# A reordered product list in a Gated DeltaNet stage: one z product in the front, z ahead of keys early, later first recurrences, closer inverse steps

## The chip, the core and the metric

The kernel runs on one core of a Trainium2 chip, as one launch. The metric is the device time in microseconds (us) of the whole program. TensorE does the matrix products, VectorE, ScalarE and GpSimd the work on tiles, and SyncE issues the DMAs.

## The reference, cut to what matters

One inference step of two layers, a Gated DeltaNet (GDN) mixer and an RWKV-7 mixer, over 1,104 tokens (64 sample tokens in 8 sequences of 8, 16 meta tokens, 1,024 prompt tokens) with a model width of 1,024. The change touches the GDN layer alone:

```python
proj = xn @ w_in                               # q, k, v, z and two gates
qkv, new_buf = causal_conv(qkv, conv_buf, conv_w)   # width 4, then SiLU
q, k = l2norm(q) * 128 ** -0.5, l2norm(k)      # 8 heads of 128, each for two v heads
L = where(strict, (beta * k) @ k.T * decay, 0) # per chunk and head
sol = triangular_solve(L + I, rhs)             # the inverse, block by block
v_new = u - w @ S                              # recurrence over the chunks
o = (q * exp(gc)) @ S + attn @ v_new
S = S * exp(g_last) + k_dec.T @ v_new
o = rmsnorm(o) * silu(z)                       # then the output projection
```

## The kernel before

**The work.** The tokens lie in three segments (384, 384, 336). A *product* multiplies them with one 128-column block of `w_in`. Each weight and each input is split into a high and a low part, so a product has 3 segments x 8 row blocks x 3 matmuls = 72 matmuls. There are 48 of them: for each of eight head groups j one for keys (k), one for queries (q), two for values (v) and two for the gate z.

**The slots.** `product` yields after 12 matmuls, half a segment: that is a *slot*, six per product, 288 in all. `layer0` drives the generator `products` and, behind each slot, calls whatever `gdn_events` planned for a time up to the next slot (`before`). TensorE and ScalarE run strictly in this written order (`manual_schedule`). VectorE, GpSimd and SyncE are ordered by the framework's scheduler, which takes the written order as priority.

**A convolved product** (k, q, v; `conv`) copies each segment out of PSUM on ScalarE, takes three taps and a SiLU on VectorE and stores it. **A z product** (`gdn_gate`) has one tanh on ScalarE and one VectorE operation per segment, and keeps the tile `zg`, of which there are six.

**The front of a group** (`front_events`, `gdn_prep`): decay tables by DMA (`decay`), their exponentials, the score products k k^T and their scaling on VectorE (`scores`), the 32x32 diagonal blocks through memory into `invA` (`blocks`), then 31 steps of two VectorE operations each that invert all 72 blocks at once (`steps`, `inverse32`). Then `spread`: a transposing copy, two DMAs out to memory (`g_u`, `g_t`) and DMAs back into `T1n` and `TT`. Then four merges (`merges`) that put the blocks together to 64 and 128 on TensorE; the first, `y32`, reads `T1n`.

**The recurrence of a group** (`chain_events`, `gdn_recur`): begun at slot a = `first[j]`, 26 steps at one per slot over nine tiles of 128 tokens. The merges stand at a - 6.5, a - 4.5, a - 3.5 and a - 1.5; the normalised and gated output leaves at a + 14.5 to a + 31.5, in three parts and two heads (`gdn_norm_out`), which frees `zg`.

**The order before.** Group 0's k, q, v, v fill slots -24 to 0. Then each stretch j = 1 to 7 of 36 slots is k(j), z(j-1), z(j-1), q(j), v(j), v(j), and the last two z follow. `first` is 9, 43, 78 and then every 36. In a stretch with base b, b + 18 is where q starts (`qb`). The 15 pairs of inverse steps stand one slot apart (`inv`), `spread` at a - 9.9.

Of the kernel before, what the change touches and what calls it, by code (L numbers as in the profile page):

```python
# [22 lines left out]
NEG = -1.0e30  # L23
ZF = 1
QF = 0


class Ctx:
# [7 lines left out]
class Builder:  # L36
# [589 lines left out]

    def gdn_queries(self, j, G, xh, xl, after=None):
        def dst(s):
            G.Q[s] = self.t(self.kp, [128, 384], "Q", 4)
            return G.Q[s]  # L630
        return self.product(128 * j, "q", xh, xl, self.conv(G.H, 1, j, dst), after)

# [213 lines left out]
    def gdn_recur(self, j, G):  # L846

        nc, t, gp, tc = self.nc, self.t, self.gp, self.tc
        col = self.col
        S = t(gp, [128, 2, 128], "S", 2)  # L850
        hv = lambda h: 2 * j + h
        hs = (0, 1)
        G.seg = {}
        for tg in range(9):
            s, tt = divmod(tg, 3)
            TT, bv = G.TT[s], G.bv[s]
            k, q = G.K[s][:, 128 * tt:128 * tt + 128], G.Q[s][:, 128 * tt:128 * tt + 128]
            if tt == 0:
                G.seg[s] = [], t(gp, [128, 3, 2], "ssq", 2)
            os, ssq = G.seg[s]  # L860
            o = t(gp, [128, 2, 128], "o", 6)
            os.append(o)

            e = [col[:, tg, 2, hv(h):hv(h) + 1] for h in hs]
            X, w = [t(gp, [128, 128], "X", 2) for h in hs], [t(gp, [128, 128], "w", 5) for h in hs]
# [24 lines left out]
            for h in hs:  # L890
                if tg == 0:
                    self.mm(part(h, 2), kt[64:128, h], w[h][64:128])
                else:
                    self.mm(part(h, 2), kt[:, h], w[h])
            for h in hs:
                self.mm(part(h, 0), at[:, tt, h], w[h])
            with tc.high_priority():
                for h in hs:
                    if tg == 0:
                        nc.vector.tensor_copy(S[:, h], part(h, 2))  # L900
                    else:
# [12 lines left out]
            G.squares = lambda o=o, ssq=ssq, tt=tt: [self.act(t(gp, [128, 128], "ojunk", 1, BF16), o[:, h], AF.Square, accum=ssq[:, tt, h:h + 1])  # L914
                                                     for h in hs]
            if tg == 8:
                nc.sync.dma_start(self.o["p_gdn"][0, 0, 2 * j:2 * j + 2].rearrange("h k v -> k h v"), S)
            yield

    def gdn_events(self, G, open_, gate, swap):  # L920

        self.events = {}
        base = [36 * (j - 1) for j in range(9)]
        first = [9, 43] + [base[j + 1] + 6 for j in range(2, 8)]
        for u in (-22.9, -19.4, -16.8, -16.7, -16.6):
            self.at(u, gate)
        self.at(-13, swap)
        for j in range(8):
            self.chain_events(j, G, first[j])
            if j:  # L930
                self.front_events(j, G, base[j], base[j] + 18, first[j], open_, base[j] + max(0.3, first[j - 1] - base[j] - 3.4))
            else:
                self.front_events(0, G, -24, -18, first[0], None, None)

    def at(self, u, f, *a):
        self.events.setdefault(u, []).append(lambda: f(*a))
# [58 lines left out]
    def front_events(self, j, G, b, qb, a, open_, e):  # L995

        g, at = lambda: G[j], self.at
        Sb = {}
# [3 lines left out]

        def read(h):
            self.gdn_sample_read(g(), h, [Sb[h, q] for q in (0, 1)])
        va = qb + 6
        at(b + 0.1, lambda: self.gdn_prep(j, g()))
        if j:
            at(b - 5.7, open_, j)
            at(b - 1.4, lambda: self.history_turn(g().H))
            k = max(b + 5.5, e + 4.7)  # L1010
            ed, ee, es = [e + 2 * s for s in range(3)], [k + 2 * s - 1.8 for s in range(3)], [k + 2 * s for s in range(3)]
            inv, per, kk, ss, rd = [k + 9.3 + n for n in range(15)], 2, (b + 11.8, qb + 4.2), b + 13.2, (qb + 6.4, qb + 9.9)
            sp = a - 9.9
        else:
            ed, ee, es = [-18.5, -18.4, -18.3], [-16, -15.2, -14.4], [-15.2, -14.4, -13.6]
            inv, per, kk, ss, rd = [-11.5 + n for n in range(10)], 3, (-12.2, -12.1), -12.8, (-7.6, -4.1)
            sp = -1
        for s in range(3):
            at(ed[s], lambda s=s: g().decay(s))
            for tt in range(3):  # L1020
# [1101 lines left out]
    def layer0(self, top, right, xa, xc):  # L2122
# [36 lines left out]
        self.gdn_events(G, open_, lambda: next(gate, None), swap)  # L2159

        def products():
            yield from G[0].keys(0)
            yield from self.gdn_queries(0, G[0], kh, kl, 2048)
            yield from self.gdn_values(0, G[0], 0, kh, kl, 2176)
            yield from self.gdn_values(0, G[0], 1, kh, kl, 1152)
            for j in range(1, 8):
                k = 128 * (j + 1)
                z = [4096 + 256 * (j - 1), 4224 + 256 * (j - 1)]
                va = 2048 + 256 * j
                yield from G[j].keys(z[0])  # L2170
                yield from self.gdn_gate(j - 1, G[j - 1], 0, kh, kl, z[1])
                yield from self.gdn_gate(j - 1, G[j - 1], 1, kh, kl, 128 * j)
                yield from self.gdn_queries(j, G[j], kh, kl, va)
                yield from self.gdn_values(j, G[j], 0, kh, kl, va + 128)
                yield from self.gdn_values(j, G[j], 1, kh, kl, 1024 + k if j < 7 else 4096 + 256 * 7)
            yield from self.gdn_gate(7, G[7], 0, kh, kl, 4224 + 256 * 7)
            yield from self.gdn_gate(7, G[7], 1, kh, kl)

        def before(u):
            while True:  # L2180
# [2 lines left out]
                    return  # L2183
                for f in self.events.pop(v):
                    f()
        before(-24)
        with tc.manual_schedule(engines={mybir.EngineType.PE, mybir.EngineType.Activation}):
            self.slot = -24
            for _ in products():
                before(self.slot + 1)  # L2190
                self.slot += 1
# [8 lines left out]
        free = [t(self.kp, [128, 384], n, b) for n, b in (("K", 6), ("K", 6), ("Q", 4))]  # L2200
# [341 lines left out]
```

## Time and profile before

| what | us |
|---|---|
| runs shown, median of three | 2196.59 (2194.4 to 2201.57) |
| the profiled execution, whole | 2193.46 |
| its span, first to last instruction | 2191.7 |
| mean granted TensorE clock | 0.979 |
| first key product starts | 44.9 |
| keys of group 1 start | 113.4 |
| keys of group 2, 3, 4 start | 255.3, 391.4, 510.6 |
| last two z products start | 987.1 |

The profile is of one execution. A row of a timeline gives the start, the time taken, engine, source line, operation, output <- inputs, and in brackets the idle time before it with what ended it. A row of windows gives the length of the stretch, then the busy time (and instructions) of TensorE's matmuls, its weight loads, VectorE, ScalarE and GpSimd, then the granted clock, the busy share of the DMA engines, and GB/s. A row of waits gives the waiting engine and tile, the releaser, the sum in us, how often and the longest. A row of groups gives the count, the busy time, the mean in ns of one, and the idle time before. Tile names carry the kernel's names: `rY` is a merge product, `dk`, `dq`, `dv`, `dz` the projections, `E` a decay table, `invT` and `invtmp` the inverse, `cvy` the convolution.

### The profile page before, as it was taken

The page shows a single profiled execution, that of the slowest core. Times are in us where ns is not written, and L with a number is a line of the kernel's source. Part 1 is how long each engine was busy: PE and PEld are TensorE (multiplying, and loading weights), DVE is VectorE, ACT ScalarE, POOL GpSimd, SP SyncE. Part 2 cuts the span into 40 slices and gives each one's busy share as a digit, 9 for nine tenths or more (in the row PEclk, how much of TensorE's full clock was granted, in tenths as well). Part 3 has the DMA queues.
Part 4 walks back from the last instruction along what each step waited for, and adds up shares of the span by engine and source line. Part 5 has one row for each costly group of instructions (what it writes and reads, how often), then busy time and mean ns, then how long its engine had stood idle before and what let it go on. Part 6 is the DMA issues. An engine that isn't in the chain of part 4 may idle for free. (4 is left out here: it accounts for less than half of the span.)

```text
span 2191.7 us, 54812 instructions
## 1 busy us (share of the span) xinstructions
PE 2051.0 (94%) x20404; PEld 1908.7 (87%) x20404; DVE 1588.0 (72%) x4221; ACT 1291.8 (59%) x3761; POOL 844.7 (39%) x1125
## 2 busy tenths in 40 slices
PE   6869899999999999999899999889999999999997
PEld 5859799899999999999899999889888988888876
DVE  7967869788887979695334676757969657767755
ACT  5526466656566565656633365664847446777774
POOL 3423333334333333334231362344534344444444
PEclk9979999999999999999999999899999999999998
DMA  4423342333333433335345215655555376677764
GB/s 118 119 58 90 86 111 78 102 90 97 104 105 97 112 83 103 110 98 145 121 125 128 67 53 190 211 168 173 171 168 163 115 222 174 180 229 226 234 178 136
DMA packets 430661, 292.64 MB, mean 134 GB/s; under 512 B 147146, under 2 KB 412987, under 8 KB 430395
## 3 DMA queue, kind: packets, MB, share of 16 engines
q1 hardware_dynamic: 430394, 289.14, 45.9%
q8 instruction: 161, 2.64, 0.5%
q14 instruction: 106, 0.86, 0.1%
HBM read 197.68 MB, written 91.37 MB: 132 GB/s over the span
## 5 line engine op out<-in xcount | busy, mean ns | idle before, releaser
L90 POOL TENSOR_TENSOR wlo<-wraw,whi 128x512 fp32r<-128x512 f32 (+1 forms) x246 | 330.6, 1346 | 469.5 <-ACT whi L86 434.9
L76 PE MATMUL d<-xc,whi 128*128 128x384 f32 (+2 forms) x1006 | 279.7, 336 | 4.6 <-ACT whi L86 3.9
L523 DVE SCALAR_TENSOR_TENSOR cvy<-raw,cw,cvy 128x408 f32<-128x408 f32 (+2 forms) x288 | 192.5, 669 | 20.3 <-ACT cvy L62 18.8
L86 ACT CAST whi<-wraw 128x512 fp32r<-128x512 f32 (+1 forms) x246 | 149.7, 611 | 86.4 <-PE d L76 48.8
L76 PEld LDWEIGHTS d<-xc,whi 128*128 128x128 f32 (+1 forms) x1006 | 183.2, 189 | 7.4 <-ACT whi L86 4.6
L76 PE MATMUL d<-xc,wlo 128*128 128x384 f32 (+3 forms) x476 | 157.4, 339 | 2.6 <-POOL wlo L90 2.6
L76 PE MATMUL dz<-xc,whi 128*128 128x384 f32 (+1 forms) x480 | 153.7, 338 | 0.0
L76 PE MATMUL dv<-xc,whi 128*128 128x384 f32 (+1 forms) x480 | 152.2, 337 | 0.0
L76 PE MATMUL d<-xa,whi 128*128 128x384 f32 (+3 forms) x450 | 143.2, 342 | 1.6 <-DVE xb L1160 1.2
L62 ACT ACTIVATE o<-rA,gcol 128x128 f32<-128x128 f32 x128 | 42.1, 366 | 117.6 <-DVE S L902 117.3
L570 DVE TENSOR_TENSOR invtmp<-invA,invT 72x31 f32<-72x31 f32 (+15 forms) x248 | 102.5, 413 | 3.2
L76 PE MATMUL dv<-xa,whi 128*128 128x384 f32 (+1 forms) x288 | 99.0, 344 | 0.0
L572 DVE TENSOR_TENSOR invT<-invT,invtmp 72x31 f32<-72x31 f32 (+15 forms) x248 | 96.1, 388 | 3.3
L76 PE MATMUL dz<-xa,whi 128*128 128x384 f32 (+1 forms) x288 | 98.5, 342 | 0.0
L76 PEld LDWEIGHTS d<-xc,wlo 128*128 128x128 f32 (+1 forms) x476 | 89.2, 189 | 6.3 <-POOL wlo L90 3.5
L76 PEld LDWEIGHTS dz<-xc,whi 128*128 128x128 f32 x480 | 89.3, 188 | 4.6 <-issue 4.6
L76 PEld LDWEIGHTS dv<-xc,whi 128*128 128x128 f32 x480 | 89.1, 188 | 1.4 <-issue 1.4
L76 PEld LDWEIGHTS d<-xa,whi 128*128 128x128 f32 (+1 forms) x450 | 85.2, 192 | 4.8 <-issue 3.3
L76 PE MATMUL d<-xa,wlo 128*128 128x384 f32 (+3 forms) x252 | 85.6, 340 | 1.4 <-POOL wlo L90 1.4
L76 PE MATMUL dq<-xc,whi 128*128 128x384 f32 (+1 forms) x240 | 78.0, 342 | 3.0 <-ACT whi L86 3.0
L76 PE MATMUL dk<-xc,whi 128*128 128x384 f32 (+1 forms) x240 | 78.6, 347 | 0.0
L62 ACT ACTIVATE mixs<-xb,omu 128x64 f32<-128x64 f32 (+3 forms) x128 | 61.6, 521 | 18.3 <-DVE xc L90 8.6
(523 smaller groups left out, 6829.5 us busy)
## 6 DMA issues: line engine op xcount, KB each, us to landing
wraw<-in_gdn_w_in SPq DMA_DIRECT2D x96, 256.0 KB
wraw<-in_rwkv_w_rkvz SPq DMA_DIRECT2D x80, 256.0 KB
Sb<-in_state_gdn SPq DMA_DIRECT2D x64, 256.0 KB
sldcak<-cakd SPq DMA_DIRECT2D x24, 576.0 KB
wraw<-in_rwkv_w_o SPq DMA_DIRECT2D x42, 256.0 KB
E<-drow SPq DMA_DIRECT2D x24, 384.0 KB
attn<-drow SPq DMA_DIRECT2D x24, 384.0 KB
wraw<-in_gdn_w_out SPq DMA_DIRECT2D x36, 256.0 KB
```

The source lines that it names most:

```text
L62: return self.nc.scalar.activation(out, in_, func, bias=bias, scale=scale, **kw)
L76: self.nc.tensor.matmul(out, lhsT, rhs, start=start, stop=stop)
L86: nc.scalar.copy(hi, x)
L90: e.tensor_tensor(lo, x, hi.bitcast(F32), op=ALU.subtract)
L523: nc.vector.scalar_tensor_tensor(y[0][:, 0:wd], raw[:, k:k + wd], cw[k], y[0][:, 0:wd], op0=ALU.mult, op1=ALU.add)
L570: nc.vector.tensor_tensor(tmp, A[:, j, j + 1:32].unsqueeze(2).broadcast_to([nb, n, m]), Tv[:, j, 0:m].unsqueeze(1).broadcast_to([nb, n, m] ...
L572: nc.vector.tensor_tensor(Tv[:, j + 1:32, 0:m], Tv[:, j + 1:32, 0:m], tmp, op=ALU.subtract)
```

## The change

The list of products is written as strings, one per group: k, q, v, w (the second v), x and y (the two z of the group before), X and Y (the two z of this one).

```diff
+ORDER = ("kqXvw", "ykqvw", "xkyqvw", "xkyqvw", "kxyqvw", "kxyqvw", "kxyqvw", "kxyqvwXY")
@@ gdn_queries, gdn_recur: buffers
-            G.Q[s] = self.t(self.kp, [128, 384], "Q", 4)
+            G.Q[s] = self.t(self.kp, [128, 384], "Q", 5)
-            o = t(gp, [128, 2, 128], "o", 6)
+            o = t(gp, [128, 2, 128], "o", 5)
-            ..., [t(gp, [128, 128], "w", 5) for h in hs]
+            ..., [t(gp, [128, 128], "w", 4) for h in hs]
@@ gdn_events
-        base = [36 * (j - 1) for j in range(9)]
-        first = [9, 43] + [base[j + 1] + 6 for j in range(2, 8)]
-        for u in (-22.9, -19.4, -16.8, -16.7, -16.6):
+        base = [-30]
+        for j in range(8):
+            base.append(base[j] + 6 * min(len(ORDER[j]), 6))
+        first = [12, 45, 78.5, 112, 146, 180.5] + [base[j + 1] + 6 for j in range(6, 8)]
+        for u in (-28.9, -25.4, -22.8, -22.7, -22.6):
             self.at(u, gate)
-        self.at(-13, swap)
+        self.at(-19, swap)
@@ front_events: b base, a = first[j], a0 = first[j - 1]
+        kb, qb, va, vb = (b + 6 * ORDER[j].index(c) for c in "kqvw")
         if j:
-            k = max(b + 5.5, e + 4.7)
+            e = max(kb + 0.3, a0 - 3.4)
+            k = max(kb + 5.5, e + 4.7)
             ed, ee, es = [e + 2 * s for s in range(3)], [k + 2 * s - 1.8 for s in range(3)], [k + 2 * s for s in range(3)]
-            inv, per, kk, ss, rd = [k + 9.3 + n for n in range(15)], 2, (b + 11.8, qb + 4.2), b + 13.2, (qb + 6.4, qb + 9.9)
-            sp = a - 9.9
+            if j < 8:
+                inv, per = [k + 8.7 + 0.85 * n for n in range(15)], 2
+                sp = max(k + 9 + 15 * 0.85, a0 + 17.2)
+                ss = max(kb + 6, a0 + 3.3)
+                kk = max(kb + 5.3, b + 11.8), qb + 4.2
+                u = max(qb + 6.4, a0 + 9.5)
+                rd = u, u + 3.5
...
         else:
-            ed, ee, es = [-18.5, -18.4, -18.3], [-16, -15.2, -14.4], [-15.2, -14.4, -13.6]
-            inv, per, kk, ss, rd = [-11.5 + n for n in range(10)], 3, (-12.2, -12.1), -12.8, (-7.6, -4.1)
-            sp = -1
+            ed, ee, es = [-24.5, -24.4, -24.3], [-22, -21.2, -20.4], [-21.2, -20.4, -19.6]
+            inv, per, kk, ss, rd = [-12.5 + 0.9 * n for n in range(10)], 3, (-18.2, -18.1), -18, (-13.6, -10.1)
+            sp = -2
...
-        for h in (0, 1):
+        for h, v in ((0, va), (1, vb)):
             for s in range(3):
-                at(va + 6 * h + 5.4 + 2 * s, lambda h=h, s=s: self.gdn_value_rows(g(), h, s))
-        at(va + 12.95, lambda: self.last_tokens(j, g().H))
+                u = max(v + 5.4 + 2 * s, a0 + 9 * s + 5.8 + 0.2 * h if 0 < j < 8 else -99)
+                at(u, lambda h=h, s=s: self.gdn_value_rows(g(), h, s))
+        at(max(qb, vb) + 6.95, lambda: self.last_tokens(j, g().H))
@@ layer0: products() walks ORDER, each product naming the next one's weights
-        before(-24)
+        before(-30)
```

By slots: the front has 30 slots (k, q, X, v, w) instead of 24, stretch 1 has 30 (y, k, q, v, w) instead of 36, the others 36, and the z of group 7 follow as before: 288 in both. Counted from the first key slot, the eight recurrences begin at 33, 67, 102, 138, 174, 210, 246, 282 before, and at 42, 75, 108.5, 142, 176, 210.5, 246, 282 after. In stretches 2 and 3 one z product stands ahead of k. The inverse steps of groups 1 to 7 stand 0.85 slots apart and begin 8.7 slots behind the first score (before 1 and 9.3). Memory of the buffers is the same in sum. What is computed, and each product's own code, is unchanged.

More of the change, by code (lines that the diff above doesn't have):

```diff
@@ L860, in gdn_recur @@
             os, ssq = G.seg[s]
-            o = t(gp, [128, 2, 128], "o", 6)
+            o = t(gp, [128, 2, 128], "o", 5)
             os.append(o)
             e = [col[:, tg, 2, hv(h):hv(h) + 1] for h in hs]
-            X, w = [t(gp, [128, 128], "X", 2) for h in hs], [t(gp, [128, 128], "w", 5) for h in hs]
+            X, w = [t(gp, [128, 128], "X", 2) for h in hs], [t(gp, [128, 128], "w", 4) for h in hs]
             r = [self.ps("r", 3, "A") for h in hs]
@@ L922, in gdn_events @@
         self.events = {}
-        base = [36 * (j - 1) for j in range(9)]
-        first = [9, 43] + [base[j + 1] + 6 for j in range(2, 8)]
-        for u in (-22.9, -19.4, -16.8, -16.7, -16.6):
+        base = [-30]
[3 more added lines that the diff above has]
+        for u in (-28.9, -25.4, -22.8, -22.7, -22.6):
             self.at(u, gate)
-        self.at(-13, swap)
+        self.at(-19, swap)
         for j in range(8):
             self.chain_events(j, G, first[j])
[L930 to L933, printed above, removed]
+            self.front_events(j, G, base[j], first[j], first[j - 1] if j else None, open_)
     def at(self, u, f, *a):
@@ L993, in chain_events, with front_events @@
                 at((14.5, 23.5, 30.5)[s] + h, lambda s=s, h=h: self.gdn_norm_out(j, G[j], s, h))
-    def front_events(self, j, G, b, qb, a, open_, e):
+    def front_events(self, j, G, b, a, a0, open_):
         g, at = lambda: G[j], self.at
@@ L1009, in front_events @@
             at(b - 1.4, lambda: self.history_turn(g().H))
-            k = max(b + 5.5, e + 4.7)
+            e = max(kb + 0.3, a0 - 3.4)
+            k = max(kb + 5.5, e + 4.7)
             ed, ee, es = [e + 2 * s for s in range(3)], [k + 2 * s - 1.8 for s in range(3)], [k + 2 * s for s in range(3)]
-            inv, per, kk, ss, rd = [k + 9.3 + n for n in range(15)], 2, (b + 11.8, qb + 4.2), b + 13.2, (qb + 6.4, qb + 9.9)
-            sp = a - 9.9
-        else:
-            ed, ee, es = [-18.5, -18.4, -18.3], [-16, -15.2, -14.4], [-15.2, -14.4, -13.6]
-            inv, per, kk, ss, rd = [-11.5 + n for n in range(10)], 3, (-12.2, -12.1), -12.8, (-7.6, -4.1)
-            sp = -1
+            if j < 8:
[5 more added lines that the diff above has]
+                rd = u, u + 3.5
+            else:
+                inv, per, kk, ss, rd = [k + 9.3 + n for n in range(15)], 2, (b + 11.8, qb + 4.2), b + 13.2, (qb + 6.4, qb + 9.9)
+                sp = a - 9.9
+        else:
+            ed, ee, es = [-24.5, -24.4, -24.3], [-22, -21.2, -20.4], [-21.2, -20.4, -19.6]
+            inv, per, kk, ss, rd = [-12.5 + 0.9 * n for n in range(10)], 3, (-18.2, -18.1), -18, (-13.6, -10.1)
+            sp = -2
         for s in range(3):
@@ L2161, in products @@
         def products():
[L2162 to L2177, printed above, removed]
+            todo = []
+            for j in range(8):
+                for c in ORDER[j]:
+                    if c == "k":
+                        todo.append((1024 + 128 * j, lambda w, j=j: G[j].keys(w)))
+                    elif c == "q":
+                        todo.append((128 * j, lambda w, j=j: self.gdn_queries(j, G[j], kh, kl, w)))
+                    elif c in "vw":
+                        h = "vw".index(c)
+                        todo.append((2048 + 128 * (2 * j + h), lambda w, j=j, h=h: self.gdn_values(j, G[j], h, kh, kl, w)))
+                    else:
+                        h = "xyXY".index(c)
+                        i, h = j - 1 + h // 2, h % 2
+                        todo.append((4096 + 128 * (2 * i + h), lambda w, i=i, h=h: self.gdn_gate(i, G[i], h, kh, kl, w)))
+            for n, (_, f) in enumerate(todo):
+                yield from f(todo[n + 1][0] if n + 1 < len(todo) else None)
         def before(u):
@@ L2185, in before @@
                     f()
-        before(-24)
+        before(-30)
         with tc.manual_schedule(engines={mybir.EngineType.PE, mybir.EngineType.Activation}):
-            self.slot = -24
+            self.slot = -30
             for _ in products():
@@ L2199, in layer0 @@
         sb = [t(sp, [128, 512], f"stage{k}") for k in range(2)]
-        free = [t(self.kp, [128, 384], n, b) for n, b in (("K", 6), ("K", 6), ("Q", 4))]
+        free = [t(self.kp, [128, 384], n, b) for n, b in (("K", 6), ("K", 6), ("Q", 5))]
         ga, gb = self.load_split(free, self.ogd[0:8], kh, kl), self.residual_in(sb, xb)
```

1 line of the change is left out of this document (removed).

## The prediction

> **What bounds the kernel now.** I read the page first, then the stretches between key products, then TensorE's waits, then the timeline at those waits.
>
> ```profile
> span 2191.7 us, 54812 instructions
> ...
> PE 2051.0 (94%) x20404; PEld 1908.7 (87%) x20404; DVE 1588.0 (72%) x4221; ACT 1291.8 (59%) x3761; POOL 844.7 (39%) x1125
> ...
> PE   6869899999999999999899999889999999999997
> ```
>
> TensorE is busy 94% of the span, so the change can only win where it idles. In the row of 40 slices of 54.8 us the third digit (110 to 164 us) is a 6 and the fifth an 8, inside the GDN stage that the change reorders. The windows cut the GDN stage at the start of each key product. They hold the front of 24 slots, two early stretches of 36 slots, and four of the five later ones.
>
> ```profile
> 44.90:113.40 68.50, 61.38 (x417) 58.04 (x416) 57.66 (x149) 35.83 (x92) 27.01 (x45) 0.98 0.36 96
> 113.40:255.30 141.90, 119.14 (x1018) 113.32 (x1016) 108.50 (x308) 70.78 (x229) 42.46 (x65) 0.92 0.30 79
> 255.30:391.40 136.10, 121.12 (x1094) 115.41 (x1092) 104.72 (x300) 78.47 (x263) 50.88 (x73) 0.95 0.36 95
> 391.40:510.60 119.20, 117.98 (x1023) 112.59 (x1021) 96.05 (x276) 70.70 (x233) 41.94 (x63) 0.99 0.35 97
> 510.60:630.10 119.50, 117.43 (x1025) 111.08 (x1021) 101.24 (x280) 74.36 (x246) 44.08 (x66) 1.00 0.36 99
> ```
>
> Equal work takes 141.9 and 136.1 us early and 119.2 us later: together 39.6 us too long. A slot of the settled part is 119.2/36 = 3.31 us. The waits of TensorE name the cause, in 80 to 420 us and then around the second and third place:
>
> ```profile
> PE rY L76 <- DMA T1n<-g_t: 32.7, 6, 20.1
> ...
> PE rY L76 <- DMA T1n<-g_t: 9.1, 2, 8.6
> ...
> PE rY L76 <- DMA T1n<-g_t: 3.1, 2, 2.5
> ```
>
> All 32.7 us is one wait, for the first merge product of chains 0, 1 and 2 (20.6 + 9.1 + 3.1): it needs the inverse of the 32x32 blocks, spread by DMA. TensorE's timeline there, then at chain 4 for comparison:
>
> ```profile
> 121.24 0.49 PE L73 MATMUL fss<-ident,Q 128*128 128x128 f32 x3
> 141.83 0.31 PE L76 MATMUL rY<-T1n,E 32*32 32x32 f32 x2 [20.10 <-DMA T1n<-g_t]
> 142.66 2.12 PE L76 MATMUL rY<-T1n,E 32*32 32x32 f32 x70 [0.52 <-DMA T1n<-g_t]
> ...
> 145.52 0.52 PE L76 MATMUL dk<-xa,whi 128*128 128x384 f32 x1
> 145.84 0.52 PE L76 MATMUL dk<-xc,whi 128*128 128x384 f32 x1
> ...
> 388.52 0.28 PE L76 MATMUL rY<-T1n,E 32*32 32x32 f32 x2 [2.51 <-DMA T1n<-g_t]
> 389.35 2.12 PE L76 MATMUL rY<-T1n,E 32*32 32x32 f32 x70 [0.55 <-DMA T1n<-g_t]
> 391.40 0.69 PE L76 MATMUL dk<-xa,whi 128*128 128x384 f32 x1
> ...
> 395.05 0.27 PE L73 MATMUL flast<-ident,last 128*108 128x128 f32 x1
> ...
> 628.83 1.33 PE L76 MATMUL rY<-T1n,E 32*32 32x32 f32 x72
> 630.37 0.34 PE L76 MATMUL dk<-xa,wlo 128*128 128x384 f32 x1
> ```
>
> After each stall the matmuls run slowly: they start 0.32 us apart (145.52, 145.84) where 0.17 is usual, and the merge takes 2.12 us, not 1.33. In the third place twelve matmuls take 391.40 to 395.05 = 3.65 us, not 2.1. That is 1.5 + 0.8 = 2.3 us behind each stall, some 7 us for three. Stalls and slow clock make 39.7 us, which meets the 39.6 of the stretches: **39.7 us is the most this change can take away.**
>
> Now why the inverse is late: VectorE and the DMA queue, in chain 0 and in chain 4.
>
> ```profile
> 98.11 0.19 DVE L570 TENSOR_TENSOR invtmp<-invA,invT 72x31 f32<-72x31 f32 x1
> ...
> 136.33 0.19 DVE L572 TENSOR_TENSOR invT<-invT,invtmp 72x31 f32<-72x31 f32 x1
> 136.55 1.03 DVE L740 COPY invA<-invT 72x1024 f32<-72x1024 f32 x1
> ...
> 261.04 1.02 DVE L740 COPY invA<-invT 72x1024 f32<-72x1024 f32 x1
> ...
> 136.54 0.27 SPq L743 DMA_DIRECT2D g_t<-invT  x1
> ...
> 139.38 1.40 SPq L746 DMA_DIRECT2D T1n<-g_t  x3
> ...
> 621.61 0.18 DVE L572 TENSOR_TENSOR invT<-invT,invtmp 72x31 f32<-72x31 f32 x1
> 622.27 1.12 DVE L740 COPY invA<-invT 72x1024 f32<-72x1024 f32 x1
> ```
>
> The tail from the last step to the last merge operand is 142.66 - 136.54 = 6.1 us, fixed by two DMAs in series. In chain 4 the steps end at 621.8; plus 6.1 is 627.9, and TensorE arrives at 628.83. The settled stretches are only 0.9 us from stalling too.
>
> ```profile
> 98.20:113.40 15.20, 15.06 (x120) 14.10 (x119) 14.79 (x40) 7.69 (x21) 5.04 (x7) 1.00 0.37 98
> ...
> 142.70:257.60 114.90, 113.57 (x981) 108.18 (x981) 87.72 (x257) 68.51 (x226) 37.47 (x57) 0.97 0.33 88
> ...
> 98.20:137.60 39.40, 22.58 (x163) 21.02 (x161) 37.86 (x98) 12.17 (x34) 9.79 (x13) 0.84 0.21 56
> ...
> 571.10:622.30 51.20, 50.06 (x383) 48.15 (x383) 48.57 (x138) 31.97 (x108) 15.66 (x26) 1.00 0.27 79
> ```
>
> In both inverses (chain 0 in 98.2 to 137.6, chain 4 in 571.1 to 622.3) VectorE, the third column after the length, is 96% and 95% busy. The inverse waits its turn among convolutions, not on anything idle.
>
> **The change part by part.** No product, recurrence or DMA is added or removed: 48 products, 288 slots. It moves them. Costs on VectorE, from the groups of 510.6 to 630.1 us (one stretch: four convolved products, two z products):
>
> ```profile
> L523 DVE SCALAR_TENSOR_TENSOR cvy<-raw,cw,cvy 128x336 f32<-128x336 f32 (+2 forms) x36 | 24.1, 670 | 2.1 <-ACT cvy L62 2.0
> L570 DVE TENSOR_TENSOR invtmp<-invA,invT 72x31 f32<-72x31 f32 (+15 forms) x31 | 13.7, 441 | 0.4
> L572 DVE TENSOR_TENSOR invT<-invT,invtmp 72x31 f32<-72x31 f32 (+15 forms) x31 | 12.1, 390 | 0.4
> ...
> L1065 DVE SCALAR_TENSOR_TENSOR zg<-mog,hgn,zg 128x384 f32<-128x384 f32 (+1 forms) x6 | 3.6, 593 | 0.1
> ...
> L831 DVE SCALAR_TENSOR_TENSOR zg<-zg,dz 128x384 f32<-128x384 f32 (+1 forms) x6 | 3.2, 532 | 2.1 <-ACT zg L62 2.1
> ```
>
> A convolved product costs 24.1/4 = 6.0 us of taps plus some 2 us of SiLU, so 8; a z product 3 x 0.53 = 1.6; an inverse 13.7 + 12.1 = 25.8.
>
> *Chain 0.* Before, first merge at slot 9 - 6.5 = 2.5, 27 product slots after the first key. After, at 12 - 6.5 = 5.5 with a front of 30: 36 slots. The nine extra are a z product inside the front (X) and the z product y where three slots of the next keys stood. TensorE's arrival: 121.7, plus X, plus y instead of three key slots. A v product without recurrences took 15.2 us (row 98.2 to 113.4), and 72 bare matmuls at 0.17 are 12.2; I take 14 for a z product. The three key slots took 8.3 (113.4 to 121.7). Arrival 121.7 + 14 + 14 - 8.3 = 141.4. VectorE: keys, decays and scores keep their places from the start, so the blocks land at 98 as now. What it did from 98.2 to 137.6 was 37.9 us; the key segment (2.7) goes out, five us of v convolution that ran before 98 come in, and three z updates (1.6): 41.8 at 96% is 43.5 us, copy done at 141.7, last step 140.6, operands 146.7. Stall 5.3 us. If the last segment and a half of v convolutions (4 us) fall behind the steps it is 1.3; if none of the steps catches a gap, 8. I take 5, plus 2.3 of clock: 7.3 in place of 20.6 + 2.7.
>
> The Trainium skill, in "TensorE: Matmul & The Clock Gate", Part 1, says that the clock halves after an idle window of about 3.4 us and recovers after a busy one. The third stall was 2.5 + 0.6 us with a short merge between, and the matmuls behind it were slow all the same, so the trace bites somewhat earlier; by the page alone a stall of 1.3 would cost only itself, and a 5 us one the clock too, as I have it.
>
> *Chains 1 and 2.* Their merges come at 45 - 6.5 = 38.5 and 72 (before 36.5, 71.5). The product last in line under the inverse is now x, with 1.6 us of VectorE, where a v product (8) stood: 6.4 us less ahead of the spread. Chain 1: TensorE reached its merge at 266.98 - 9.1 - 0.3 = 257.6, and the copy ran at 261.04. From merge 0 (142.7) to 257.6 VectorE was busy 87.7 us, idle mostly at the start. With 3.3 more to the copy that makes some 91; the change takes off two z products (3.2), adds the moved key segment (2.7) and a backlog of up to 5 from chain 0: some 95. TensorE's way is 33 slots at 3.31, 109 us, less 6.1 of tail: 103. The 95 take 100 at the 95% that VectorE reached, so it just fits. Scores to merge is one slot shorter (3.3 us). I take a rest of 1 us for both; bounds 0 and 6.
>
> *Steps at 0.85 of a slot, spread later.* For chains 3 to 6 the scores-to-merge distance shrinks (24.2 slots to 21.7, 22.2, 22.7, 23.7), but the 15 pairs of steps take 2.1 slots less, and the planned spread now stands 4 to 4.9 slots ahead of the merge, not 3.4: at least 13 us against 6.1 of tail plus VectorE's lag behind the plan, which was about 1 us in chain 4 (planned behind the third slot of the last v product, some 621.6; copy 622.27). The steps need 25.8 us of some 39, the rest of VectorE's work in that time was 0.45 per us, so it is oversubscribed by some 4 us: still inside. Cost taken 0, bounds -1 and 7 per chain.
>
> *z products early.* x of stretch 2 stands at slots 30 to 36 and needs a third gate buffer by slot 35; chain 0 frees its third at 12 + 23.5 = 35.5. The ScalarE tanh waits for the gate update (0.59), and an output DMA (g_t to T1n, 2.84, is nearest): some 4 us. Behind it on ScalarE stand chain 0's w scalings and the copies that free TensorE's accumulators; two slots of products lie between, so I charge 1 us (0 to 6). Buffers o 6 to 5 and w 5 to 4: each is freed half a slot or more ahead of its next write; Q gains one. 1 us for all other waits.
>
> **Sum.** 39.7 - 7.3 - 1 - 1 - 1 = 29 us off the profiled execution's own 2193.5 (span 2191.7): **2164**. The median of the runs shown is 2196.6, three us above that execution; 2164 stays my figure, between.
>
> **Rivals.**
> 1. *VectorE keeps the bound in the front* (chance 0.17). The 96% row speaks for it: chain 0 stalls 8 to 12 us, chains 1 and 2 keep half of theirs (6 + 4 of clock). Gives 39.7 - 14 - 10 - 3 = 13 us: 2181.
> 2. *The step pace does not follow; slower* (0.09). If scores to merge stays fixed in time, chains 3 to 6 miss by 2.5, 2, 1.5 and 0.5 slots less 0.9 us: 7.4 + 5.7 + 4.1 + 0.8 = 18, with clock 25; chains 1 and 2 keep 12.2 and lose 1 and 1.5 slots more (8.3), with clock 25; chain 0 keeps 7.3. That is 57 against 39.7: 2211. It decides at a VectorE demand 5 us above the window in q, v, w. The 95% row and the 0.9 us speak for it, the 18 us that VectorE idles per stretch and the wider spread gap against.
> 3. *ScalarE held by the gate buffer* (0.05): the mechanism above, at full price with clock, 4 + 2.3 more: 2170. The Trainium skill, same page and part ("Engine queue depths"), calls ScalarE's queue strictly first in, first out, so nothing overtakes that tanh; here its order is written out in any case.
> 4. *Gains cancel* (0.07): rivals 1 and 2 in part; within 6 us of now.
>
> **Numbers.** The forecast has 0.62. Faster by over 0.3% (about 6.6 us, what a measurement of this kernel can tell from no change): 0.62 + 0.17 + 0.05 = 0.84; within 0.3%: 0.07; slower: 0.09. The range reaches from nearly all of 39.7 gained with a good run (2151) past rival 1 with its bounds (2190).
>
> **What would show it.** The six T1n waits fall from 32.7 to under 10, the largest in chain 0 and at most 8; granted clock in the first two stretches near 0.98; the stall of chains 1 and 2 gone; later stretches (36 slots) at 119 to 122 us with no T1n wait. Wrong if chains 3 to 6 show T1n waits of over 2 us, if ScalarE sits several us at a z tanh in stretch 2 with TensorE idle behind it, or if VectorE's steps in chain 0 end after 143.

## The result, and the profile after

| | before | after |
|---|---|---|
| median of five runs, us | 2196.71 (2194.4 to 2201.57) | 2212.39 (2206.26 to 2223.7) |
| profiled execution, whole | 2193.46 | 2215.11 |
| mean granted clock | 0.979 | 0.976 |

The ratio after to before is 1.0075, 95% interval 1.0056 to 1.0094: **slower by 15.7 us**, where 2164 was forecast. Lines of the code stand one or ten further down in the profile after.

The page after: its span, and TensorE's row of the 40 slices (55.3 us each).

```profile
span 2213.4 us, 54815 instructions
...
PE   5989998998989999999899999899998999999997
```

The 6 in the third slice became an 8, as meant. But 8s stand in the seventh, tenth and twelfth slice too: the one deep hole became several shallow ones. The windows of the GDN stage, cut at the same numbers of products as those shown of before (stretches 1 to 4 and 7, then the whole stage of 46 products), with the whole stage of before in the fence behind:

```profile
114.50:244.40 129.90, 114.67 (x965) 108.78 (x962) 100.53 (x274) 67.29 (x211) 44.47 (x70) 0.93 0.31 82
244.40:375.80 131.40, 121.42 (x1045) 116.37 (x1042) 106.40 (x305) 78.99 (x264) 43.33 (x67) 0.96 0.34 90
375.80:498.40 122.60, 118.81 (x1044) 113.23 (x1042) 96.58 (x286) 77.25 (x253) 42.12 (x67) 1.00 0.35 94
498.40:636.90 138.50, 124.03 (x1044) 118.48 (x1043) 104.27 (x301) 75.03 (x250) 43.41 (x65) 0.94 0.34 93
...
883.00:1004.10 121.10, 117.18 (x1026) 111.27 (x1019) 97.75 (x278) 73.76 (x243) 42.53 (x63) 1.00 0.39 107
...
45.30:1004.10 958.80, 895.27 (x7622) 852.05 (x7620) 763.67 (x2144) 556.84 (x1799) 327.40 (x506) 0.97 0.35 94
```

```profile
44.90:987.10 942.20, 888.11 (x7622) 843.39 (x7620) 768.25 (x2144) 553.66 (x1797) 336.01 (x506) 0.98 0.35 96
```

The first two full stretches fell from 141.9 and 136.1 to 129.9 and 131.4, as meant. But the third rose from 119.2 to 122.6, the fourth from 119.5 to 138.5, and the last from 119.2 to 121.1. In all the stage is 16.6 us longer with the same 7622 matmuls: 7.2 of it are matmuls that ran longer (895.27 against 888.11, at a lower clock), 9.4 are idle time (63.5 against 54.1). That is close to the 15.7 of the medians. The two profiled executions differ by 21.7; the other 5 us lie nearly all behind the stage.

Which idle time grew? TensorE's waits from 40 to 1060 us, before (the row of T1n, 32.7, stands in the prediction) and after:

```profile
PE rA L76 <- DVE o L913: 5.5, 10, 0.9
PE rA L76 <- DVE S L902: 3.2, 7, 0.9
```

```profile
PE rY L77 <- DMA T1n<-g_t: 19.0, 7, 8.3
PE mhist L74 <- ACT ktok L63: 10.1, 2, 6.5
PE rA L77 <- DVE o L914: 8.3, 14, 1.1
...
PE rA L77 <- DVE S L903: 3.7, 7, 1.2
...
PE mhist L74 <- DVE zg L1075: 2.8, 1, 2.8
```

T1n lost 13.7 us, not the 27 forecast. **A wait that the prediction did not look at is new:** `mhist`, 12.9 us in three places. And the recurrence's own waits for S and `o` from VectorE (`rA`) grew from 8.7 to 12.0. First T1n, on TensorE's timeline at chains 0 and 3:

```profile
141.50 0.31 PE L77 MATMUL dz<-xc,whi 128*128 128x336 f32 x1
150.09 0.28 PE L77 MATMUL rY<-T1n,E 32*32 32x32 f32 x2 [8.28 <-DMA T1n<-g_t]
...
517.25 0.31 PE L77 MATMUL rY<-T1n,E 32*32 32x32 f32 x2 [6.82 <-DMA T1n<-g_t]
518.20 2.02 PE L77 MATMUL rY<-T1n,E 32*32 32x32 f32 x68 [0.65 <-DMA T1n<-g_t]
```

Chain 0 went nearly as forecast: arrival 141.8 for 141.4, stall 8.3 for 5. Chain 3 was to have none, and has 7.5. Now `mhist`: the product turns the saved last rows of a group, planned at b - 1.4 (`history_turn`), and its accumulator is the one PSUM bank of the tag `m`. In groups 2, 3 and 5 the new starts of the recurrences put it straight behind a key-token product or a gated output, which use the same bank. The longest wait, all engines in order of time:

```profile
361.91 0.60 PE L77 MATMUL rA<-w,ktok 128*128 128x128 f32 x4
...
363.13 0.27 PE L74 MATMUL mktok<-ident,K 128*128 128x128 f32 x1
363.36 0.17 DVE L111 TENSOR_TENSOR on_t<-ors 128x6 f32<-128x6 f32 x1 [1.21 <-POOL ors L103]
...
365.86 0.41 DVE L571 TENSOR_TENSOR invtmp<-invA,invT 72x255 f32<-72x255 f32 x1
366.19 0.59 DVE L903 SCALAR_TENSOR_TENSOR S<-S,eglb,rA 128x128 f32<-128x128 f32 x2
366.56 0.63 ACT L63 ACTIVATE o<-rA,gcol 128x128 f32<-128x128 f32 x2 [4.67 <-DVE S L903]
...
369.26 0.62 ACT L63 ACTIVATE ktok<-mktok,gcol 128x128 f32<-128x128 f32 x2
...
369.93 0.42 PE L74 MATMUL mhist<-ident,hist 96*128 96x96 f32 x1 [6.53 <-ACT ktok L63]
```

The matmul for the state S was through at 362.5. VectorE stood idle until 363.36 for a small GpSimd result (`ors`), then did inverse steps and convolutions, and updated S at 366.19. ScalarE runs in its written order: `o` stands behind S with 4.67 us of idle time, several operations later follows the copy `ktok` that empties the bank, and TensorE waits 6.5 for that. So a bank is what TensorE waits for, and VectorE's lateness is behind it: of the 3.7 us by which S was late, about 0.9 was VectorE waiting itself.

### The profile page after: what moved, and what is told of

It is laid out like the page before. It is cut to its first block, busy times and chain, and to the rows that moved or that the text cites. A ratio compares the mean times of both kernels' runs of the same rounds, so it can differ in the third digit from the quotient of the medians.

```text
span 2213.4 us, 54815 instructions
## 1 busy us (share of the span) xinstructions
PE 2059.4 (93%) x20404; PEld 1917.7 (87%) x20404; DVE 1583.1 (72%) x4221; ACT 1293.5 (58%) x3761; POOL 835.4 (38%) x1125
## 5 line engine op out<-in xcount | busy, mean ns | idle before, releaser
L571 DVE TENSOR_TENSOR invtmp<-invA,invT 72x31 f32<-72x31 f32 (+15 forms) x248 | 99.1, 400 | 15.6 <-DMA invA<-ltd 12.6
L573 DVE TENSOR_TENSOR invT<-invT,invtmp 72x31 f32<-72x31 f32 (+15 forms) x248 | 90.8, 366 | 3.4
L63 ACT ACTIVATE mixs<-xb,omu 128x64 f32<-128x64 f32 (+3 forms) x128 | 61.7, 521 | 17.6 <-DVE xc L91 8.4
```

The source lines that it names most:

```text
L63: return self.nc.scalar.activation(out, in_, func, bias=bias, scale=scale, **kw)
L571: nc.vector.tensor_tensor(tmp, A[:, j, j + 1:32].unsqueeze(2).broadcast_to([nb, n, m]), Tv[:, j, 0:m].unsqueeze(1).broadcast_to([nb, n, m] ...
L573: nc.vector.tensor_tensor(Tv[:, j + 1:32, 0:m], Tv[:, j + 1:32, 0:m], tmp, op=ALU.subtract)
```

## The experiments

Two theories were held against each other. **The pace theory:** VectorE's pace sets the loop from merge to merge, so a wait that is taken away comes back at the next place that needs VectorE. **The bank theory:** what the change gains is given back at `m`'s bank, and would be there without that collision. The expectations call their theories A, B and so on, each in its own sense. Ratios are to the kernel before; the edits are made to the changed kernel unless it says otherwise.

**Buffers alone** (kernel before, the three buffer counts of the change).

> The kernel before with the change's buffer counts alone (Q 5, o 5, w 4). If the smaller buffers cost something, slower than before by 2 us or more with new waits at o or w; I expect no difference, within 3 us of before.

2200.66, ratio 1.0001 (0.9981 to 1.0022). The buffers cost nothing that these runs can tell.

**The history turn one slot later, in groups 2, 3 and 5.**

```diff
-at(b - 1.4, lambda: self.history_turn(g().H))
+at(b - (0.4 if j in (2, 3, 5) else 1.4), lambda: self.history_turn(g().H))
```

> The changed kernel with one event moved: the turn of the convolution history in groups 2, 3 and 5 stands one slot later (b - 0.4, not b - 1.4), so that it no longer stands directly behind a user of the same PSUM bank (key tokens at 28.5 and 64.5, a gated output at 136.5). Theory A (single bank m): TensorE's waits for the history turn, 3.6 + 6.5 + 2.8 = 12.9 us, go, with some 6 us of half clock behind them: 18 us less than the changed kernel, about 2194. Theory B (VectorE is the bound, the bank only shows it): TensorE loses the same time at the next reader of VectorE or of bank m, under 6 us less, 2206 or more.

2224.9, 1.0115 (1.0084 to 1.0147). The waits of `mhist` fell to 1.0 us, and those of T1n rose by 12.4. The same with the collision removed at its root, in its old place:

```diff
-p = self.ps("m", 1, "hist")
+p = self.ps("f", 2, "hist")
```

> The changed kernel with the history turn in the tag f with its two banks in place of the one bank of m, in its own place and nothing else. Theory A (the collision at the bank costs its 12.9 us plus clock): 2195 to 2202 us, stage about 945. Theory B (VectorE is late, so that the wait moves to T1n, as it did when the turn was moved by one slot): 2210 to 2225, stage 955 to 968, with T1n waits of 25 us and more.

2225.03, 1.012 (1.0092 to 1.0148), and no wait of `mhist` at all. T1n in TensorE's waits, 31.4 us with the moved turn, and with the other bank:

```profile
PE rY L77 <- DMA T1n<-g_t: 32.7, 11, 8.2
```

12.9 us of one wait became 12 to 14 us of another. The reading is that VectorE caught up with its inverse while TensorE stood at `mhist`, and that TensorE without that pause meets the inverse unfinished: both expectations named this outcome as their theory B. With the full work the pace theory holds, in that the wait comes back. It does not say why both kernels are some 12 us slower than the change, and not equal to it. In the profiled execution with the other bank the stage takes 967.8 us, 9.0 more than in the change; 6.2 of that is idle time and 2.8 are longer matmuls. The T1n waits are more numerous (11, not 7) and those of `rA` for S and `o` are 15.7; why, these runs do not settle.

**Two taps less.** This kernel leaves out the second and third tap of every convolution, so VectorE has less to do and TensorE the same. It does not compute the whole convolution; it tests VectorE's load alone.

```diff
-for k in range(1, 4):
+for k in range(3, 4):
```

> The changed kernel with the convolution's second and third tap left out (24 instead of 36 of every stretch's tap operations go: 16 us of VectorE per stretch). If the steps are held by VectorE's load (it is 93 to 97% busy from first to last step), they shrink from 52 to 56 us to under 45, the T1n waits of chains 1 to 7 vanish, and the time falls by 30 us or more, below 2180. If only positions and latencies hold them, steps stay at 50 or more and the time within 10 us of 2212.

2151.26, 0.9781 (0.9752 to 0.981). The same edit in the kernel before:

> The kernel before with the convolution's second and third tap left out, the control to the changed kernel with the same (2151.3). Theory V (VectorE's load turns the change's gain into waits): with a light VectorE the change gains what was forecast for it, so this one stands 15 to 30 us above 2151, at 2166 to 2181. If the light VectorE helps both alike, this one is at 2140 or below, and the change is bad for another reason.

2149.69, 0.9777 (0.9745 to 0.9808). Both gain far more than the change was to bring, and they are equal. The control lies between the two values expected for it: VectorE's load explains the change's loss, which is gone here, but not why the change still brings no gain. The leading waits of the changed kernel, then of the kernel before, with two taps less:

```profile
PE mhist L74 <- ACT ktok L63: 8.0, 2, 5.2
```

```profile
PE rY L76 <- DMA T1n<-g_t: 18.3, 6, 13.9
```

With a lighter VectorE the change does take T1n to nothing, and still gains nothing: now `mhist` and its like stand where T1n was. Is it the bank this time? Both edits together:

> The changed kernel with two of the three taps of every convolution left out (the second and third), and the history turn in the tag f with its two banks in place of the one bank of m. With the taps alone the changed kernel took 2151.3 us and the kernel before with the taps left out 2149.7: the change gained nothing although its T1n waits were gone (18.3 us to 0). Theory A (the one bank of m is what gives the gain back): the 9.3 us of mhist waits and the clock behind them go, stage 885 to 892 us, 2135 to 2143, ratio to before about 0.973. Theory B (any wait that is taken away comes back at the next place that TensorE waits for ScalarE or VectorE): 2147 to 2153, ratio about 0.978, with the waits of rA, mktok and f up by as much.

2141.04, 0.9741 (0.9717 to 0.9765). The leading waits that are left:

```profile
PE rA L77 <- DVE o L914: 5.2, 13, 0.8
```

The bank theory holds here: 10 us less than with the bank shared, 8.7 less than the kernel before with the same taps (which has no such wait in its rows). The ends of the intervals overlap a little, 0.9752 and 0.9745 against 0.9765, and each kernel has four runs. **So the bank matters once VectorE keeps up, and removing it does harm while VectorE doesn't.** The order of the change is worth some 9 us to a kernel whose VectorE has room, as far as these few runs tell.

The loop shows why. The first 32-merge of chain 7 in the kernel before and in the change, then those of chains 0 and 7 in the change with fewer taps and the other bank, and in the kernel before with fewer taps:

```profile
985.87 1.33 PE L76 MATMUL rY<-T1n,E 32*32 32x32 f32 x72
```

```profile
1002.88 1.33 PE L77 MATMUL rY<-T1n,E 32*32 32x32 f32 x72
```

```profile
137.35 0.82 PE L77 MATMUL rY<-T1n,E 32*32 32x32 f32 x40
...
936.33 1.33 PE L77 MATMUL rY<-T1n,E 32*32 32x32 f32 x72
```

```profile
131.61 0.31 PE L76 MATMUL rY<-T1n,E 32*32 32x32 f32 x2 [13.89 <-DMA T1n<-g_t]
...
943.16 1.33 PE L76 MATMUL rY<-T1n,E 32*32 32x32 f32 x72
```

Before, seven periods took 985.87 - 141.83 = 844.0 us. After, 1002.88 - 150.09 = 852.8, though the plan gives them nine slots less (240, not 249). The forecast needed about 957 - 147 = 810 (29 us earlier at the end, first merge at 147). With VectorE light the change's order and the other bank take 936.33 - 137.35 = 799.0. The old order with VectorE light takes 943.16 - 131.61 = 811.6. So most of the shortening is VectorE's load, and the order of the change with the other bank adds 12.6 us to it; with its full work VectorE delivers neither.

**The steps as before** (one slot apart, 9.3 behind the score, spread at a - 9.9 or later).

```diff
-inv, per = [k + 8.7 + 0.85 * n for n in range(15)], 2
-sp = max(k + 9 + 15 * 0.85, a0 + 17.2)
+inv, per = [k + 9.3 + n for n in range(15)], 2
+sp = max(a - 9.9, a0 + 17.2)
```

> The changed kernel with the inverse steps of groups 1 to 7 one slot apart, 9.3 behind the first score, and the spread 9.9 ahead of the recurrence, as before. If the closer steps serve to keep the merges in time, the T1n waits of chains 1 to 6 rise from 10.7 to 30 us or more (2230); if the closer steps crowd VectorE and delay what TensorE waits for (history turn, rA), the sum stays or falls (2212 or less).

2233.22, 1.0164 (1.0135 to 1.0194), with the T1n waits at 37.2: the shorter periods need the closer steps. But closer steps have a price of their own. The kernel before with the 0.85 spacing and its spread:

> The kernel before with the closer inverse steps alone (0.85 of a slot apart, first 8.7 behind the first score, spread 21.75 behind it). If the closer steps help by themselves, the T1n waits of chains 1 and 2 (9.1 and 3.1 us with their clock) shrink and the time falls by 5 to 12 us. If VectorE has no room (97% busy under the steps of chain 1), nothing changes within 4 us.

2203.21, 1.0021 (1.0 to 1.0043): slower at the very edge of what the runs can tell, although T1n fell from 32.7 to 28.5. A settled stretch of it; the kernel before takes 118.9 to 119.5 there:

```profile
507.40:628.90 121.50, 117.59 (x1026) 111.28 (x1021) 98.67 (x280) 74.17 (x246) 44.02 (x66) 1.00 0.35 97
```

Two us are lost in this stretch, and in the one two further on (121.4). TensorE's `rA` waits for S and `o` rise from 8.7 to 14.9 us in all and those of `f` for `vt` from 1.8 to 5.4; that the steps now stand ahead of these operations on VectorE is the likely reason. The other side is to put the steps of groups 6 and 7 alone back, with their spread and keys' rows:

```diff
-if j < 8:
+if j < 6:
```

> The changed kernel with the inverse steps (one slot apart, 9.3 behind the score), the spread and the keys' rows of groups 6 and 7 in the places of the kernel before; the products and recurrences there have those places in both kernels. The stretches of groups 6 and 7 (between first key products) take 123.6 and 121.1 us in the change, 119 in the kernel before, with rA and f waits of 2.5 and 1.3 against 1.2 and 0.3. Theory A (the closer steps crowd the recurrence's VectorE operations in every settled stretch): both come to 119 to 120, rA under 1.5 each, 2206 to 2208. Theory B (lateness carried over from the stretches ahead): they stay at 121 to 124, and the time within 2210 to 2215.

The stretches of groups 6 and 7 in the profiled execution:

```profile
758.20:880.10 121.90, 117.93 (x1096) 111.83 (x1094) 103.97 (x284) 75.41 (x247) 46.59 (x72) 1.00 0.38 103
880.10:998.80 118.70, 117.13 (x1023) 111.08 (x1019) 99.03 (x283) 73.81 (x242) 40.48 (x62) 1.00 0.38 102
```

The last one fell from 121.1 to 118.7, that of before, as theory A has it; the one ahead of it only from 123.6 to 121.9, as theory B has it. The median, 2213.0 (1.007, 1.0046 to 1.0095), lies where theory B put it, and the profiled execution, 2202.1, was the fastest of six. That the closer steps cost some 2 us in a stretch is seen in single executions; a gain from putting two of them back is not shown.

**Other orders.** The z products of stretches 2 and 3 behind the keys again (`ORDER[2]` and `[3]` "kxyqvw"):

> The changed kernel with stretches 2 and 3 in the order k x y q v w, one z product no longer ahead of the keys. If the light z product under the end of the inverse is what keeps chains 1 and 2 from stalling, their T1n waits come back (now 0.6 and 0), by 5 us or more each, and the time rises to 2220 or more; if it does nothing there, the time stays within 4 us of 2212.

2219.87, 1.0085 (1.0053 to 1.0117): no better, no clear loss. The T1n wait of chain 1 came back by 2.5 us (0.6 to 3.1), that of chain 2 not at all, so the early z product does little there. Recurrences spread evenly, `first` = 12, 48, 84, 119, 154, 189, 224, 260, z ahead of keys throughout, the turn in `f`:

> The changed kernel with the recurrences 36, 36, 35, 35, 35, 35, 36 slots apart (12, 48, 84, 119, 154, 189, 224, 260) instead of 33 to 36; for this the stretches 2 to 7 are x k y q v w, and the history turn uses the two-bank tag f. Theory L (a loop from merge to merge: y32, scores, blocks, steps, spread, y32, takes 119 to 124 us whatever the slots): with 36 slots planned the merges of chains 2 to 7 wait little, their periods are 119 to 121, the last first-merge comes near 990 (1003 now) and the recurrence of group 7 ends with fewer products beside it: 2195 to 2203. Theory P (TensorE-bound, spacing only places the work): the same work, chain 7 eight slots later with nothing beside it, slower by 10 us or more, over 2220.

2218.02, 1.0076 (1.0048 to 1.0104). The kernel before with q ahead of the second z (k x q y v w):

> The kernel before, with first recurrences, inverse steps and front of before, and the products of the stretches in the order k x q y v w in place of k x y q v w, so that VectorE's convolutions are spread more evenly; the buffers Q, o, w as in the change. Theory A (waits come from bursts of VectorE's work): T1n waits of chains 1 and 2 (12.1 us) fall by half, 2185 to 2190. Theory B (the spare time of VectorE in a whole stretch decides, not its order within): 2194 to 2205.

2206.16, 1.0035 (1.0019 to 1.0052): T1n at 33.2, as before, and the `rA` waits for S and `o` at 18.4, not 8.7. These last two times lie just outside the nearer of their two forecasts (theory P, theory B). None of the three orders gains.

**Towards a better version.** Scores half a slot to a slot sooner (`k` = max(kb + 5.5, e + 3.7), 1.5 slots between segments, steps from k + 7.7), so that the inverse starts earlier:

> The changed kernel with the scores of groups 1 to 7 sooner behind the decay loads (first score 3.7 slots behind, not 4.7, the three 1.5 slots apart, not 2) and steps and spread moved along with them, two slots in all. Theory L: first merge to scaled scores falls from 50 to some 44 us, periods of chains 1 to 5 from 121-125 to 115-119, T1n waits of 1 to 5 go: 2190 or less. Theory V (VectorE's throughput alone): the steps begin sooner and take as much longer; no gain, 2205 or more.

2210.17, 1.0053 (1.0034 to 1.0072): T1n fell to 8.5 us, but `rA` now waits 15.2 for S and `o` and 3.9 for ScalarE's `w`. With the turn in `f` as well:

> The kernel of the sooner scores, and the history turn in the two-bank tag f, so that it no longer waits for key tokens. Theory L: alone the moved history turn gave nothing because the merge waited instead; with the loop shortened, its 13 us count, and this is faster than the sooner scores alone by 5 us or more (2185 or less).

2208.45, 1.0036 (1.0015 to 1.0057), far from the 2185 expected. And with VectorE's work cut, the value scaling and the copies of the merges going to ScalarE (shortened: the copies of the 32-merges go the same way):

```diff
-nc.vector.tensor_tensor(G.bv[s][:, :, h, :], ...)
+for tt in range(3):
+    self.act(G.bv[s][:, tt, h, :], ..., AF.Identity, scale=...)
-nc.vector.tensor_copy(Ys[64:128], ...)
+nc.scalar.copy(Ys[64:128], ...)
```

> The changed kernel with sooner scores and the two-bank history turn, and some 7 us per stretch of VectorE's work given to ScalarE: the scaling of the value rows (bv, 3.8 us) and the copies of the merge products Y (3.6 us). What is computed stays. Theory V: a relief of 7 of the 16 us that the left-out taps gave is worth about half of their gain, 20 us: 2190 or below. If VectorE's load is not what matters, no gain, 2205 or more.

2199.71, 0.9997 (0.9981 to 1.0013), the best of the change with its full work: level with the kernel before, between the two values expected. Its waits:

```profile
PE rA L77 <- DVE S L903: 8.7, 12, 1.7
...
PE rA L77 <- ACT w L63: 7.7, 6, 5.4
```

ScalarE is late now (`w`, up to 5.4 us). The same relief in the kernel before:

> The kernel before with the same relief of VectorE (value rows and merge copies on ScalarE). Its settled stretches are bound by TensorE, so only the early three stalls (39.7 us with the clock) can shrink: I expect 5 to 12 us less than before, 2187 to 2193; nothing if the steps do not follow.

2207.77, 1.0033 (1.0014 to 1.0051): worse by itself, where a gain was expected. T1n fell from 32.7 to 26.8, but TensorE's waits for `vt` (tile `f`) rose from 1.8 to 14.0. And the best variant with the steps of groups 6 and 7 as before:

> The best variant so far (scores half a slot to a slot sooner, history turn in the tag f, value scaling and merge copies on ScalarE; 2199.7 us) with the steps, spread and rows of groups 6 and 7 as in the kernel before. Theory A: the last two stretches lose some 2 us each, 2194 to 2197. Theory B: no change, 2198 to 2202.

2204.5, 1.0025 (1.0007 to 1.0043): no faster, where theory A expected a gain. No version with its full work beat the kernel before.

## Why the prediction was wrong

- **What bounds the kernel: right, but one-sided.** The 39.7 us are what the three stalls cost, and the inverse on VectorE is what TensorE waits for there. No such sum was made for what the change can lose, and a kernel whose settled stretches are "only 0.9 us from stalling" can lose in every one.
- **Chain 0: nearly right.** Arrival 141.8 for 141.4, stall 8.3 for 5, 0.3 us past its upper bound.
- **Chains 1 and 2: T1n right (0.6 us for 1), the conclusion not.** They were met in time after TensorE had stood at `mhist` for 3.6 and 6.5 us. With the other bank, which takes these stalls away, they wait 5.6 and 6.0 us for T1n.
- **"Steps at 0.85 of a slot, spread later ... Cost taken 0": this is the step that failed.** It took the steps to follow the plan, 2.1 slots less per inverse. Chain 3's inverse, as a window, by its costliest groups on VectorE, and the taps in the window of chain 4 before:

```profile
455.70:511.30 55.60, 52.91 (x407) 50.76 (x407) 53.10 (x155) 37.18 (x129) 17.39 (x29) 1.00 0.26 74
```

```profile
L524 DVE SCALAR_TENSOR_TENSOR cvy<-raw,cw,cvy 128x336 f32<-128x336 f32 (+2 forms) x24 | 14.8, 615 | 0.0
L571 DVE TENSOR_TENSOR invtmp<-invA,invT 72x31 f32<-72x31 f32 (+15 forms) x31 | 12.2, 394 | 0.3
L573 DVE TENSOR_TENSOR invT<-invT,invtmp 72x31 f32<-72x31 f32 (+15 forms) x31 | 11.4, 367 | 0.2
```

```profile
L523 DVE SCALAR_TENSOR_TENSOR cvy<-raw,cw,cvy 128x408 f32<-128x408 f32 (+2 forms) x19 | 11.4, 601 | 0.0
```

  The plan gave the steps 39 us. The prediction set 25.8 us of steps and 0.45 us per us of other work against it: 25.8 + 17.6 = 43.4, "oversubscribed by some 4 us: still inside" the slack of 13 - 6.1 - 1, some 6 us. But a window that grows takes in more of the other work. At 95% busy and 0.45 taken the steps have half of VectorE, and 25.8 / 0.5 is 51.6 us, 12 over the plan and outside the slack; the row of chain 4 before, from which both shares come, shows those 51.2 us in the prediction itself. The window took 55.6: the steps' own work was 23.6 us, less than taken, but the other work was 29.5 us, 0.53 per us, with 24 taps in it and not 19. In chains 3 to 6 the steps took 51.9 to 55.6 us from first to last, against 50.7 to 51.3 before: planning them closer shortened none of these. A row that contradicts a plan was read as agreeing with it. The bound of 7 us per chain was nearly right (852.8 - 810 is 43 us in seven periods, 6 each, though not all of it at this step), but the range left it out.
- **"1 us for all other waits": wrong by some 22.** `mhist` 12.9, and all waits but it and T1n 31.6 us in place of 21.4 (idle time 63.5 - 19.0 - 12.9, and 54.1 - 32.7). The change moved several recurrences by half slots against fixed points such as b - 1.4, and which products then stand next to each other in a bank of one buffer was not looked at. With the longer matmuls, 7.2 us where a gain of some 5 was counted on, these waits are the larger part of the missed forecast; T1n of chains 1 to 6 came to 10.7 us. That VectorE's pace is behind the waits too is what the moved turn and the lighter VectorE speak for.
- **z products early: right.** ScalarE's tanh waited 4.93 us (4 forecast) for the DMA that frees the gate buffer, and TensorE went on through it without a gap, so the 1 us charged was nothing:

```profile
266.36 0.45 ACT L63 ACTIVATE zg<-dz 128x336 f32<-128x336 f32 x1 [4.93 <-DMA ogd<-zg]
```

```profile
262.00:270.00 8.00, 8.00 (x57) 8.00 (x56) 6.06 (x16) 2.51 (x11) 1.59 (x5) 1.00 0.54 144
```

- **Rival 2 was the nearest**, with its mechanism (scores to merge fixed in time) and its 2211; it had 0.09. That its figure is so close is partly luck: it put 50 us, with clock, into T1n of chains 1 to 6, which took 10.7; the rest came out at `mhist`, `rA` and other waits.
- **Signs named beforehand.** T1n under 10: 19.0. Clock near 0.98 in the first stretches: 0.93 and 0.96. Later stretches at 119 to 122: 121.1 to 138.5. T1n over 2 us in chains 3 to 6 was named as the sign of being wrong, and chains 3 (7.5) and 5 (2.4) showed it.

## What to carry to other kernels

Where the engine that is late runs at 95% in a stretch, a job spread through that stretch takes its own work divided by the share that the others leave, whatever its plan says; work out that quotient before a shorter plan is believed, and count what other work the new places bring into the stretch (0.45 us per us here became 0.53). A stall taken from the waiting engine is a gain only if the late one has room: lighten the late engine for a test (two taps less), and see whether the order then pays and which wait comes up next. When starts are moved by half slots, list for each buffer of one bank what now stands ahead of it.

## What the runs showed of the hardware

**Behind a short wait the clock was half.** In the change, TensorE waited 1.31 us ahead of three transposes, did a merge of 72 small matmuls, and then ran slowly, starts 0.32 us apart where 0.17 is usual; before, with a wait of 0.34 at the same place, it ran at full pace at once. The change, with a window of the slow matmuls (granted clock 0.50), then the kernel before:

```profile
1002.43 0.52 PE L74 MATMUL f<-ident,vt 128*128 128x128 f32 x3 [1.31 <-DVE vt L530]
...
1004.62 0.52 PE L77 MATMUL dz<-xa,wlo 128*128 128x384 f32 x1
1004.94 0.52 PE L77 MATMUL dz<-xc,whi 128*128 128x384 f32 x1
```

```profile
1004.10:1007.50 3.40, 3.40 (x18) 3.36 (x11) 3.27 (x9) 3.34 (x15) 1.54 (x3) 0.50 0.55 132
```

```profile
985.42 0.52 PE L73 MATMUL f<-ident,vt 128*128 128x128 f32 x3 [0.34 <-DVE vt L529]
...
987.40 0.33 PE L76 MATMUL dz<-xa,wlo 128*128 128x384 f32 x1
987.57 0.34 PE L76 MATMUL dz<-xc,whi 128*128 128x384 f32 x1
```

A wait of 1.31 us thus cost some 1.7 us more, half of the 3.4 at half clock. Whether the small matmuls between count as idle time, no run here separates. Such stretches are part of the 7.2 us of longer matmuls.

**GpSimd holds VectorE up.** A step of the inverse that takes 0.42 us took 1.48 while GpSimd subtracted one 128x512 tile from another (368.36 to 369.62):

```profile
361.72 0.42 DVE L573 TENSOR_TENSOR invT<-invT,invtmp 72x255 f32<-72x255 f32 x1
...
368.41 1.48 DVE L573 TENSOR_TENSOR invT<-invT,invtmp 72x252 f32<-72x252 f32 x1
```

```profile
368.36 1.26 POOL L91 TENSOR_TENSOR wlo<-wraw,whi 128x512 fp32r<-128x512 f32 x1 [2.72 <-ACT whi L87]
```

Each of the 48 products needs two such subtractions for its weights; the stage's trace has 91 of them. By the timeline, 72 VectorE operations of the stage ran over 0.5 us longer than the median of their kind, some 65 us in all, and 60 of them overlapped one of the 91 (the others another GpSimd operation). So part of VectorE's "95% busy" is time in which it is held. The Trainium skill, "SBUF — State Buffer", section "Terms", describes a port pair that VectorE and GpSimd take turns at, the loser standing still for the whole instruction; this row agrees. No run here moved the subtraction elsewhere.
